# A two-layer hybrid backbone step on one core: pre-norm by channel slices, split output-projection weights kept in SBUF, weight splits on VectorE alone, and new rules for the order

## The chip, the core and the metric

One core of a Trainium2 chip runs the whole step in one launch. The metric is device time in microseconds (us). Engines are named as in the profile: PE is TensorE (matmuls and transposes; PEld its weight loads), DVE is VectorE, ACT is ScalarE, POOL is GpSimd, SP is SyncE, which issues the DMA transfers of the weights.

## What is computed

640 tokens (512 latent tokens of a sample, 128 of a prompt) of width 1024 go through two layers. In the reference, cut to what matters here:

```python
def modulate(x, g, shift, scale):
    return rms_norm(x, g) * (1.0 + scale) + shift

for l in range(2):
    # silu(c) @ w_mod[l] + b_mod[l], cut into six sections of 1024, for sample and prompt
    mod = split(silu(c) @ w_mod[l] + b_mod[l], 6)
    h = modulate(x, norm_mix_pre[l], mod[0], mod[1])
    # layer 0: attention and Hyena on the columns of h @ w_in, joined, then @ w_out
    # layer 1: mLSTM heads, forward and backward, gated, then @ w_out
    out = mixer(h)
    x = x + mod[2] * rms_norm(out, norm_mix_post[l])
    h = modulate(x, norm_ffn_pre[l], mod[3], mod[4])
    # conv_ffn: gelu(conv(h @ w_up)[:, :2816]) * conv(h @ w_up)[:, 2816:], then @ w_down
    x = x + mod[5] * rms_norm(conv_ffn(h), norm_ffn_post[l])
```

Prompt and sample share the weights; the prompt has modulation values of its own. All is float32.

## The kernel before

**Products of split operands.** A float32 product is taken as three products of fp32r operands: each operand x is split into h, x rounded to fp32r, and l = x - h; the matmuls are h·h, l·h and h·l (`SPLIT3`, line 386). So each weight slice needs a cast (`wh`, on ACT) and a subtraction (`wl`), and each activation likewise (`a1h`, `a1l` before the first FFN; `o0h`, `o0l` before layer 0's output projection; `hh`, `hl` before a down-projection). `split` makes the pair.

**Two forms of projection.** `fm_task` and `fm_head` compute 128 output channels for all tokens, with the weight slice stationary (the up-projection of the FFN, the mLSTM's inputs): eight contraction slices k, 384 early tokens and 256 late ones. `fm_head` (line 412) begins such a phase: the early tokens of the first five outputs, then their late ones. `tm_tasks` (line 500) computes tokens by 1024 outputs, for two groups of token tiles in turn, `HALVES` = tiles 0, 1, 2, then tiles 3, 4 (a tile is 128 tokens): for each contraction slice a 512 KB weight slice is loaded, split and multiplied with each tile of the group. The last three slices (`KEEP_`) of the first group are done tile by tile and stay for the second, which begins with them; the others are loaded and split again. The output projections (eight slices) and down-projections (22 slices) have this form.

**The boundary.** When a group of a projection is done, `boundary` (line 889) is spawned as a side chain, marked urgent. It squares each tile on ACT with the sum read out, multiplies it by the modulation gate on DVE, takes the inverse root by small integer and float steps on DVE (128 by 3 elements), and adds the residual on DVE. Then `pre_norm` (line 803) normalizes again (another square and inverse root), scales each tile's row (`xn`), transposes it in blocks of 128 by 128 on PE (four to a PSUM bank), and for each block scales and shifts by channel (half on DVE, half on ACT), casts (half on DVE, half on ACT) and subtracts on POOL, all in pieces of 128 by 128. The up-projection's first matmul needs tiles 0, 1, 2 complete. A row buffer for tile 4 is one that tile 0's pre-norm has given back (line 900).

**Modulation.** `mod_section` computes a section from w_mod in 512 KB loads with ACT, DVE and POOL adding products; its `finish` folds the partitions: two DMAs, two additions on POOL (`modf`), then matmuls of two columns that add up and transpose (`modt`). Layer 1's sections 0, 1, 3, 4 and layer 0's section 5 are spawned in layer 0's FFN once hidden slice `J0` = 5 is there.

**What sets the order.** The program is emitted by a planner (`Order`, line 60). Tasks on streamed weights follow one another; side chains (boundaries, modulation, attention, Hyena, the mLSTM heads) are woven in where an estimate of each engine's time says that their operands are ready. `Lane.cost` (line 244) estimates each instruction, `issue` (line 117) keeps the engines' clocks, with 125 ns between a result and its reader on any engine. `prefetch` (line 1820) places the weights' loads and splits, one task ahead; while an urgent chain is open it gives `wl` to POOL where POOL would be free before DVE (line 1836). The three PSUM tiles `mm` and two banks `aux` are taken and given back by the same planner.

All engine calls but matmuls and transposes are recorded under one helper line, 263; matmuls are line 343, transposes line 352.

Of the kernel before, what the change touches and what calls it, by code (L numbers as in the profile page):

```python
# [18 lines left out]
P = 128  # L19
D = 1024  # L20
# [19 lines left out]
# columns of the packed per-channel vectors  # L40
# [19 lines left out]
class Order:  # L60
    """Program order. Tasks on streamed weights follow one another; side chains are woven in between, by an
    estimate of when each engine gets to an instruction and of when its operands are there. A chain yields
    nothing (go on when what it has issued is finished), a time, keys that it needs, or a PSUM tag."""

    LAT = 125.0
    TICK = 10240.0 / 3
    WARM = 1275.0
# [5 lines left out]
    def __init__(self):  # L73
# [8 lines left out]
        self.ticks = {}  # L82
        self.after = None
# [11 lines left out]
    # ---- engines  # L95
# [21 lines left out]
    def issue(self, eng, cost, outs, ins, lat=0.0, rows=1.0):  # L117
        t = max(self.t[eng], self.avail(ins) + self.LAT)
        for o in outs + [i for i in ins if str(i.space) == "PSUM"]:
            x = self.last.get(o.name)  # L120
            if x is not None and x[1] != eng:
                t = max(t, x[0] + self.LAT)
        if eng == "PE":
            q = int(t // self.TICK)
            self.ticks[q] = self.ticks.get(q, 0.0) + cost * rows
# [4 lines left out]
        f = e + lat  # L130
        for o in outs:
# [10 lines left out]
    # ---- chains  # L142
# [61 lines left out]
    def until(self, t):  # L204
        """Chains that can go on before t."""
# [16 lines left out]
    # ---- PSUM  # L222
# [15 lines left out]
class Lane:  # L238
    """An engine whose instructions are also put on the estimate."""
# [4 lines left out]
    def cost(self, op, outs, ins):  # L244
        n = 1
        for d in max(outs + ins, key=lambda a: a.free_size()).shape[1:]:
            n *= d
        psum = any(str(a.space) == "PSUM" for a in outs + ins)
        if self.key == "DVE":
            if op in ("tensor_scalar", "tensor_copy") and not psum:  # L250
                return 0.52 * n + 70 + (60 if len(ins) > 1 else 0)
            return 1.04 * n + (130 if psum else 70)
        if self.key == "ACT":
            return 0.833 * n + 95 + (145 if len(ins) > 1 else 0)
        if op == "tensor_tensor":
            return 2.3 * n + 25
        return 1.05 * n + 25

    def __getattr__(self, op):
        f = getattr(self.engine, op)  # L260

        def call(*args, **kw):
# [5 lines left out]
            if op == "dma_start":  # L268
# [3 lines left out]
                self.od.dma = max(self.od.dma, self.od.t["SP"], self.od.avail(ins)) + n / 400.0  # L272
                f_ = self.od.dma + 2000.0
# [7 lines left out]
            self.od.issue(self.key, self.cost(op, outs, ins), outs, ins)  # L281
# [1787 lines left out]
```

## Time and profile before

| | |
|---|---|
| device time, median of 3 runs | 1798.43 us (1796.11 to 1804.24) |
| profiled execution, first to last instruction | 1802.8 us |
| PE busy | 1716.3 us (95%), 10132 instructions |
| DVE busy | 1255.4 us (70%), 2052 instructions |
| ACT busy | 783.4 us (43%), 1287 instructions |
| POOL busy | 528.8 us (29%), 358 instructions |
| moved by DMA | 208.08 MB, mean 115 GB/s |

The profiled execution has no time of its own beside its span in the record; 1802.8 us lies between the median and the slowest of the three runs. Busy shares are means over stages: an engine at 70% can be what another waits for in a stretch of some microseconds. Times in the rows below are from the start of the span. A row of the timeline gives start, duration, engine, line, operation, result and operands, size, count, and in brackets how long the engine had been idle and what ended that. Matmuls overlap, so a row with x2 gives the time of both. The granted clock (PEclk) is a share of TensorE's full speed.

### The profile page before, as it was taken

The numbers are of one execution on the slowest core, as the hardware profiler recorded it, in microseconds if no ns is written. First come the engines' busy times: TensorE is split into PE (matmuls) and PEld (weight loads), VectorE is DVE, ScalarE is ACT, GpSimd is POOL, SyncE is SP. The second block draws the span as 40 slices with busy tenths as digits, with TensorE's granted clock in tenths as the row PEclk, the third lists the DMA queues.
The fourth block names the chain that finished last, engine by engine and source line by source line (L and its number), as shares of the span: only waits on it lengthen the run. The fifth ranks groups of instructions, "written<-read, shape, count | busy, mean of one in ns | idle before, by whom it ended". The sixth has DMA issues, their size and how long they took to land. (4 is left out here: it accounts for less than half of the span.)

```text
span 1802.8 us, 25891 instructions
## 1 busy us (share of the span) xinstructions
PE 1716.3 (95%) x10132; PEld 1550.6 (86%) x10132; DVE 1255.4 (70%) x2052; ACT 783.4 (43%) x1287; POOL 528.8 (29%) x358
## 2 busy tenths in 40 slices
PE   7989998998999999989899999999989999999998
PEld 3687896778999999968688999999779999998876
DVE  6777887765677798874765897787568744445465
ACT  5443235645444454433545443434465432323343
POOL 1244423125245564530612221111164412111010
PEclk9999999999999999989899999999999999999999
DMA  8334243222244444542344221212224322223343
GB/s 296 131 132 138 82 132 120 71 87 77 95 141 163 145 148 141 178 161 90 124 142 135 87 87 54 71 54 68 92 85 166 115 71 75 79 71 107 127 152 129
DMA packets 64948, 208.08 MB, mean 115 GB/s; under 512 B 7287, under 2 KB 12407, under 8 KB 64826
## 3 DMA queue, kind: packets, MB, share of 16 engines
q1 hardware_dynamic: 64826, 206.43, 34.0%
q8 instruction: 80, 1.31, 0.3%
q14 instruction: 42, 0.34, 0.1%
HBM read 200.36 MB, written 3.94 MB: 113 GB/s over the span
## 5 line engine op out<-in xcount | busy, mean ns | idle before, releaser
L263 DVE TENSOR_TENSOR wl<-wr,wh 128x1024 fp32r<-128x1024 f32 x245 | 319.8, 1307 | 151.9 <-ACT wh L263 151.8
L263 ACT CAST wh<-wr 128x1024 fp32r<-128x1024 f32 x268 | 279.8, 1046 | 226.9 <-PE dn L343 133.1
L263 POOL TENSOR_TENSOR acc<-acc,modp 128x1024 f32<-128x1024 f32 (+1 forms) x84 | 200.5, 2394 | 191.2 <-ACT modp L263 191.1
L263 POOL TENSOR_TENSOR hid<-zg,zu 128x640 f32<-128x640 f32 x44 | 106.0, 2408 | 304.1 <-DVE zu L263 304.0
L263 DVE SCALAR_TENSOR_TENSOR acc<-mw,sc,acc 128x1024 f32<-128x1024 f32 x70 | 147.9, 2113 | 17.5 <-DMA mw<-in_w_mod 16.9
L263 DVE SCALAR_TENSOR_TENSOR zg<-g,vec,zg 128x127 f32<-128x127 f32 (+3 forms) x168 | 87.3, 541 | 87.6 <-ACT zg L263 84.6
L263 POOL TENSOR_TENSOR wl<-wr,wh 128x1024 fp32r<-128x1024 f32 x23 | 56.4, 2453 | 303.6 <-ACT wh L263 297.4
L343 PE MATMUL dn<-wh,hl 128*128 128x512 f32 x440 | 140.6, 400 | 4.8 <-DVE hl L263 4.8
L343 PE MATMUL dn<-wl,hh 128*128 128x512 f32 x440 | 140.9, 401 | 3.5 <-POOL wl L263 3.5
L343 PE MATMUL dn<-wh,hh 128*128 128x512 f32 x440 | 141.1, 401 | 1.1 <-ACT hh L263 0.6
L263 DVE SCALAR_TENSOR_TENSOR zu<-u,vec,zu 128x511 f32<-128x511 f32 (+2 forms) x164 | 86.7, 549 | 79.5 <-ACT zu L263 76.6
L263 ACT ACTIVATE modp<-mw,sc 128x1024 f32<-128x1024 f32 (+1 forms) x84 | 83.6, 1009 | 117.3 <-DMA mw<-in_w_mod 66.4
L343 PE MATMUL u<-a1l,wh 128*128 128x384 f32 (+1 forms) x336 | 105.2, 313 | 3.1 <-POOL a1l L263 3.1
L343 PEld LDWEIGHTS dn<-wh,hl 128*128 128x128 f32 x440 | 83.6, 191 | 26.5 <-DVE hl L263 7.1
L343 PE MATMUL u<-a3l,wh 128*128 128x384 f32 (+1 forms) x336 | 104.5, 311 | 1.6 <-POOL a3l L263 1.6
L343 PE MATMUL u<-a1h,wl 128*128 128x384 f32 (+1 forms) x336 | 105.1, 313 | 0.4 <-DVE wl L263 0.4
L343 PE MATMUL g<-a1h,wh 128*128 128x384 f32 (+1 forms) x336 | 105.3, 313 | 0.0
L343 PE MATMUL g<-a1l,wh 128*128 128x384 f32 (+1 forms) x336 | 105.1, 313 | 0.0
L343 PE MATMUL u<-a1h,wh 128*128 128x384 f32 (+1 forms) x336 | 104.9, 312 | 0.0
L343 PE MATMUL g<-a1h,wl 128*128 128x384 f32 (+1 forms) x336 | 104.9, 312 | 0.0
L343 PEld LDWEIGHTS dn<-wl,hh 128*128 128x128 f32 x440 | 84.2, 192 | 24.0 <-POOL wl L263 4.4
L343 PE MATMUL u<-a3h,wl 128*128 128x384 f32 (+1 forms) x336 | 104.3, 310 | 0.4 <-DVE wl L263 0.4
(744 smaller groups left out, 4713.8 us busy)
## 6 DMA issues: line engine op xcount, KB each, us to landing
wr<-in_w_up SPq DMA_DIRECT2D x92, 512.0 KB, 3.6
wr<-in_w_down SPq DMA_DIRECT2D x82, 512.0 KB, 3.2
mw<-in_w_mod SPq DMA_DIRECT2D x80, 512.0 KB, 4.4
wr<-in_w_ml SPq DMA_DIRECT2D x34, 512.0 KB, 3.3
wr<-in_w_out SPq DMA_DIRECT2D x26, 512.0 KB, 3.3
wr<-in_w_in SPq DMA_DIRECT2D x13, 512.0 KB, 3.5
wr<-in_w_u SPq DMA_DIRECT2D x12, 512.0 KB, 3.1
we<-in_w_mod SPq DMA_DIRECT2D x8, 512.0 KB, 5.0
```

The lines of the kernel that those rows point to most:

```text
L263: r = f(*args, **kw)
L343: r = nc.tensor.matmul(out, lhsT, rhs, start=start, stop=stop)
```

## The change

- **Weight splits.** All `wl` go to DVE; the choice of POOL is gone from `prefetch`.
- **Output projections.** The activation is split once for all 640 tokens (`whole`), not once per group. Slices 0 to 4 in layer 0 and 2 to 4 in layer 1 (`STAY`) are split into pages of 512 columns that stay for the second group (`away`), so with the three that stayed before, layer 0 loads its eight slices once, and layer 1 loads two again. 26 loads of w_out become 18.
- **Pre-norm.** Rows are scaled in halves of 512. Then, per channel slice k, all tiles of the group are transposed to one bank and scaled, cast and subtracted as one piece of 384 or 256 columns: even k scaled on DVE, cast on ACT, subtracted on DVE; odd k scaled on ACT, cast on DVE, subtracted on POOL. Each slice is announced by itself, and the first task of the up-projection waits slice by slice (`needs`). For the first group, slice k from 3 on waits until a slice of the output projection that holds its pages is used (`FREE`).
- **Boundary.** Tile 4's row is taken from the pool `mw`, without waiting for tile 0.
- **Modulation.** `finish` lets 8000 ns pass in the estimate (`FOLDED`) between the fold on POOL and its matmuls. `J0` goes from 5 to 1.
- **mLSTM heads.** Output gates come 3 heads later, not 2 (`LAG`); of the values 2, not 3, come late (`VLAG`).
- **Order.** The estimate has new costs, a latency apart from the occupancy, a wake-up time per engine in place of 125 ns, a port that DVE and POOL take in turn for instructions on SBUF operands, and slower transfers.

Calls are recorded under lines 278, 359 and 370 now. The diff, cut:

```diff
-    LAT = 125.0
+    WAKE = {"PE": 55.0, "DVE": 40.0, "ACT": 40.0, "POOL": 80.0}
...
+        self.port = {"DVE": 0.0, "POOL": 0.0}
...
-    def issue(self, eng, cost, outs, ins, lat=0.0, rows=1.0):
-        t = max(self.t[eng], self.avail(ins) + self.LAT)
+    def issue(self, eng, cost, outs, ins, lat=0.0, act=0.0, shared=False):
+
+        t = self.avail(ins)
...
+        t = max(self.t[eng], t + self.WAKE.get(eng, 0.0))
+        if shared:
+            t = max(t, self.port["POOL" if eng == "DVE" else "DVE"])
...
+        if shared:
+            self.port[eng] = f
...
-            return 1.04 * n + (130 if psum else 70)
+            d = (0.52 if fast else 1.04) * n + 150 + 62 * ptrs
+            return (d + 25, 0, False) if op in ("tensor_reduce", "reciprocal") else (d - 85, 85, fast or len(near) > 1)
...
-            return 2.3 * n + 25
-        return 1.05 * n + 25
+            return 2.16 * n + 100, 70, True
+        return 1.0 * n + 15, 70, op != "memset"
...
-    def fm_part(out, w, act, c0, c1):
+    def fm_part(out, w, act, c0, c1, needs=None):
...
+            if needs is not None:
+                od.need([(*needs, k)])
...
-                old = g > 0 and n < KEEP
+                old = g > 0 and (n < KEEP or k in away)
+                mine = g == 0 and n in stay
+                if mine:
+                    away.add(k)
...
+                                od.ready.add((name, "used", m))
...
                 yield
+                yield FOLDED
                 yield "aux"
                 pt = aux(f"modt{l}{s}")
...
+        for c in (slice(0, 512), slice(512, D)):
+            for j, i in enumerate(tiles):
+                if j % 2:
+                    nc.scalar.mul(xn[i][:, c], xs[i][:, c], r[:, j : j + 1])
+                else:
+                    nc.vector.tensor_scalar(xn[i][:, c], xs[i][:, c], r[:, j : j + 1], None, op0=ALU.mult)
...
+        for k in range(KT):
+            yield "aux"
+            ps = aux(f"{name}t{k}")
+            for j, i in enumerate(tiles):
+                TR(ps[:, j * P : (j + 1) * P], xn[i][:, k * P : (k + 1) * P])
+            if pages is not None and tiles[0] == 0 and k >= FREE:
+                yield [(pages, "used", min(KT - 1, k - FREE + 3))]
...
+            split(h[:, c], low[:, c], y, nc.gpsimd if k % 2 else nc.vector,
+                  nc.vector.tensor_copy if k % 2 else nc.scalar.copy)
+            od.ready.add((key, l, tiles[0], k))
+            yield 0
...
             if nxt is not None and i >= ROWS:
-                yield [(key, l + (s == 5), i - ROWS)]
-            t[i] = row(f"{name}t{i}")
+                t[i] = mw.tile([P, D], F32, tag="mw", name=f"{name}t{i}")
+            else:
+                t[i] = row(f"{name}t{i}")
...
-            c0, c1 = halves[g][0] * P, halves[g][-1] * P + P
-            hh, hl = page(f"{name}h{k}{g}", FR), page(f"{name}l{k}{g}", FR)
-            split(hh[:, 0 : c1 - c0], hl[:, 0 : c1 - c0], mix[order[k]][:, c0:c1])
-            cur[g, k] = hh, hl
+            hh, hl = page(f"{name}h{k}", FR), page(f"{name}l{k}", FR)
+            split(hh[:, 0:T], hl[:, 0:T], mix[order[k]][:, 0:T])
+            cur[k] = hh, hl
...
-    LAG, VLAG = 2, 3
+    LAG = 3
+    VLAG = 2
...
-    J0 = 5
+    J0 = 1
...
-            slow = not od.urgent or max(od.t["POOL"], at) + POOLX > max(od.t["DVE"], at)
-            split(h, l, t.raw, nc.vector if slow else nc.gpsimd)
-            t.w = (h, l)
+            if t.away:
+                t.w = [[page(f"w{x}{q}{c}", FR)[:, 0:512] for c in range(2)] for x in "hl"]
+                for c in range(2):
+                    split(t.w[0][c], t.w[1][c], t.raw[:, c * 512 : c * 512 + 512])
+            else:
+                t.w = [wp.tile([P, 1024], FR, tag=f"w{x}", name=f"w{x}{q}") for x in "hl"]
+                split(*t.w, t.raw)
```

Three places show what the order becomes. First GpSimd's queue at the boundary between layer 0's output projection and its FFN (`acc` is a modulation section's sum, `wl` a weight split, `a1l` an activation split, `o0p0ny` a scaled block of the first group and `o0p3ny` of the second). Before:

```order
L263 TENSOR_TENSOR acc_2096<-acc_2096,modp_2097 128x1024 x3
L263 TENSOR_TENSOR wl_3199<-wr_3016,wh_3198 128x1024
L263 TENSOR_TENSOR wl_3223<-wr_3044,wh_3222 128x1024
L263 TENSOR_TENSOR wl_3248<-wr_3072,wh_3247 128x1024
L263 TENSOR_TENSOR wl_3287<-wr_3206,wh_3286 128x1024
L263 TENSOR_TENSOR a1l_3141<-o0p0ny_3337,a1h_3140 128x128
L263 TENSOR_TENSOR a1l_3143<-o0p0ny_3337,a1h_3142 128x128
```

With the change:

```order
L278 TENSOR_TENSOR a1l_3304<-o0p0ny_3305,a1h_3303 128x384
L278 TENSOR_TENSOR a1l_3336<-o0p0ny_3337,a1h_3335 128x384
L278 TENSOR_TENSOR a1l_3368<-o0p0ny_3369,a1h_3367 128x384
L278 TENSOR_TENSOR a1l_3406<-o0p0ny_3407,a1h_3405 128x384
L278 TENSOR_TENSOR a1l_3304<-o0p3ny_3555,a1h_3303 128x256
```

The four weight splits are gone from this queue, and four pieces per group stand where 24 and 16 stood.

Second, TensorE's queue at the same boundary (`o_3`, `o_4` are the output projection's tiles 3 and 4, `o0p0nt` the transposes of the first group). Before, with the second group's matmuls around the first transposes:

```order
L343 MATMUL o_4_3191<-wh_3247,o0l_3252 128x512 x2
L343 MATMUL o_4_3191<-wl_3248,o0h_3251 128x512 x2
L352 MATMUL o0p0nt_3332<-ident,o0p0t_3159 128x128 x4
L343 MATMUL o_3_3168<-wh_3286,o0h_3290 128x512 x2
L343 MATMUL o_3_3168<-wh_3286,o0l_3291 128x512 x2
L343 MATMUL o_3_3168<-wl_3287,o0h_3290 128x512 x2
```

With the change:

```order
L359 MATMUL o_3_3160<-wl_2914,o0h_2920 128x512
L359 MATMUL o_3_3160<-wl_2915,o0h_2920 128x512
L370 MATMUL o0p0nt_3289<-ident,o0p0t_3151 128x128
L370 MATMUL o0p0nt_3289<-ident,o0p0t_3154 128x128
L370 MATMUL o0p0nt_3289<-ident,o0p0t_3157 128x128
L370 MATMUL o0p0nt_3299<-ident,o0p0t_3151 128x128
L370 MATMUL o0p0nt_3299<-ident,o0p0t_3154 128x128
L370 MATMUL o0p0nt_3299<-ident,o0p0t_3157 128x128
L359 MATMUL o_4_3183<-wh_2912,o0h_2920 128x512
```

One tile's four blocks stood together, after 72 matmuls of tiles 3 and 4; now three tiles' blocks of one slice stand together, two slices at a time, after 66.

Third, TensorE's queue early in layer 0's down-projection (`dn_0` to `dn_2` are its first group's tiles, `modt` a modulation section's fold). Before:

```order
L343 MATMUL dn_1_6639<-wh_6484,hl_6489 128x512 x2
L343 MATMUL dn_1_6639<-wl_6485,hh_6488 128x512 x2
L343 MATMUL modt_6646<-vec,modf_6519 128x2 x8
L343 MATMUL dn_2_6664<-wh_6484,hh_6488 128x512 x2
L343 MATMUL dn_2_6664<-wh_6484,hl_6489 128x512 x2
```

With the change:

```order
L359 MATMUL dn_2_6555<-wh_6592,hl_6597 128x512 x2
L359 MATMUL dn_2_6555<-wl_6593,hh_6596 128x512 x2
L359 MATMUL modt_6676<-vec,modf_6519 128x2 x8
L359 MATMUL dn_0_6541<-wh_6620,hh_6624 128x512 x2
L359 MATMUL dn_0_6541<-wh_6620,hl_6625 128x512 x2
```

The fold's matmuls stood inside the down-projection's first slice; they stand behind its fifth now.

## Rows read from the trace of the kernel before

**Rows 1.** The page's first table: busy us (share of the span) and instructions.

```profile
PE 1716.3 (95%) x10132; PEld 1550.6 (86%) x10132; DVE 1255.4 (70%) x2052; ACT 783.4 (43%) x1287; POOL 528.8 (29%) x358
```

**Rows 2.** The per-core line: span and mean granted TensorE clock.

```profile
core 0: 1802.8 us, clock 0.977
```

**Rows 3.** Stretches: us, busy us (instructions) of PE, PEld, DVE, ACT, POOL, PEclk, DMA, GB/s.

```profile
380.00:435.00 55.00, 46.02 (x211) 38.96 (x210) 39.19 (x87) 29.26 (x58) 28.51 (x30) 0.91 0.29 96
672.00:682.00 10.00, 7.71 (x52) 7.29 (x51) 9.17 (x12) 4.89 (x6) 4.76 (x2) 1.00 0.16 54
786.00:826.00 40.00, 33.22 (x135) 27.16 (x134) 19.38 (x20) 9.84 (x14) 6.08 (x2) 0.87 0.39 117
850.00:945.00 95.00, 84.72 (x377) 68.28 (x375) 67.80 (x118) 49.29 (x88) 36.29 (x33) 0.95 0.39 129
1294.00:1330.00 36.00, 28.42 (x127) 21.45 (x126) 30.74 (x62) 22.75 (x48) 21.09 (x28) 0.95 0.36 116
1375.00:1640.00 265.00, 265.00 (x1810) 264.24 (x1809) 148.61 (x204) 91.76 (x106) 67.45 (x28) 1.00 0.27 92
75.00:200.00 125.00, 113.57 (x632) 104.93 (x631) 91.26 (x109) 52.14 (x89) 57.13 (x37) 0.93 0.40 136
```

**Rows 4.** TensorE's waits by releaser: total us, times, longest us.

```profile
PE modt L343 <- POOL modf L263: 7.2, 2, 6.8
...
PE o L343 <- DVE o0l L263: 3.8, 4, 1.7
...
PE dn L343 <- POOL wl L263: 3.5, 2, 3.3
...
PE u L343 <- POOL a1l L263: 3.1, 1, 3.1
```

**Rows 5.** VectorE's timeline at layer 0's boundary: start us, us, instruction.

```profile
382.56 2.27 DVE L263 SCALAR_TENSOR_TENSOR o0p0q<-o0p0a,o0p0q 128x3 f32<-128x3 f32 x1
...
385.32 3.35 DVE L263 SCALAR_TENSOR_TENSOR x<-o0p0t,o0p0y,x 128x1024 f32<-128x1024 f32 x1
388.60 0.41 DVE L263 TENSOR_TENSOR o0l<-vx,o0h 128x256 fp32r<-128x256 f32 x1
388.94 2.47 DVE L263 SCALAR_TENSOR_TENSOR x<-o0p0t,o0p0y,x 128x1024 f32<-128x1024 f32 x2
...
396.74 0.16 DVE L263 SCALAR_TENSOR_TENSOR o0p0ny<-o0p0na,o0p0ny 128x3 f32<-128x3 f32 x1
...
401.72 0.74 DVE L263 TENSOR_SCALAR o0p0t<-x,o0p0ny 128x1024 f32<-128x1024 f32 x1
402.39 1.21 DVE L263 TENSOR_TENSOR wl<-wr,wh 128x1024 fp32r<-128x1024 f32 x1
...
412.03 1.37 DVE L263 TENSOR_SCALAR o0p0ny<-o0p0nt,mod,mod 128x128 f32<-128x128 f32 x4 [1.09 <-PE o0p0nt L352]
```

**Rows 6.** GpSimd's timeline in the same stretch.

```profile
382.40 2.40 POOL L263 TENSOR_TENSOR wl<-wr,wh 128x1024 fp32r<-128x1024 f32 x1 [45.19 <-ACT wh L263]
385.18 2.42 POOL L263 TENSOR_TENSOR wl<-wr,wh 128x1024 fp32r<-128x1024 f32 x1 [0.38 <-ACT wh L263]
...
409.15 11.11 POOL L263 TENSOR_TENSOR a1l<-o0p0ny,a1h 128x128 fp32r<-128x128 f32 x20 [0.70 <-ACT a1h L263]
```

**Rows 7.** TensorE's timeline in the same stretch.

```profile
402.88 1.05 PE L343 MATMUL o<-wl,o0h 128*128 128x512 f32 x2
...
408.22 0.63 PE L343 MATMUL o<-wh,o0l 128*128 128x512 f32 x2
...
413.23 0.60 PE L352 MATMUL o0p0nt<-ident,o0p0t 128*128 128x128 f32 x4
```

**Rows 8.** The page's costliest groups: busy us, mean ns, idle before and its releaser.

```profile
L263 DVE TENSOR_TENSOR wl<-wr,wh 128x1024 fp32r<-128x1024 f32 x245 | 319.8, 1307 | 151.9 <-ACT wh L263 151.8
...
L263 POOL TENSOR_TENSOR wl<-wr,wh 128x1024 fp32r<-128x1024 f32 x23 | 56.4, 2453 | 303.6 <-ACT wh L263 297.4
```

**Rows 9.** ScalarE's timeline: the square that begins the chain.

```profile
379.02 1.02 ACT L263 ACTIVATE o0p0j<-o 128x1024 bf16<-128x1024 f32 x1 [3.07 <-PE o L343]
```

More of the change, by code (lines that the diff above doesn't have):

```diff
@@ L441, in run @@
                 held = w is None
[L442 removed]
+                yield from fm_part(pl[:, 0 : T - CUT], st[n, "w"] if held else w, act, CUT, T,
+                                   needs_b if n == back[0] else None)
                 if held and RB:
@@ L498, in fm_first, with tm_tasks, cols, flat @@
         return [take(n) for n in range(3)] + [Task(all_)]
-    def tm_tasks(lhs, src, nk, groups, name, finish, prep=None, needs=lambda k, g: (), single=False, tail=False, own=None, subs=(), more=()):
-        out, held = [], {}
-        KEEP = KEEP_ + bool(more)
+    def tm_tasks(lhs, src, nk, groups, name, finish, prep=None, needs=lambda k, g: (), single=False, tail=False, own=None, stay=(), whole=False):
+        out, held, away = [], {}, set()
+        def cols(w, c):
+            return w[c] if isinstance(w, list) else w[:, c * 512 : c * 512 + 512]
+        def flat(w):
+            return [x for y in w for x in (y if isinstance(y, list) else [y])]
         def group(g, order):
@@ L531, in run @@
                         held[k] = w
-                    if n == nk - 1 and not last and prep is not None:
+                    if n == nk - 1 and not last and prep is not None and not whole:
                         for m in range(nk - 1, nk - 1 - KEEP, -1):
@@ L560, in run @@
                             finish(pss[i], i)
-                        elif n == nk - 1:
-                            for sub in subs or [tiles]:
-                                if i == sub[-1]:
-                                    finish({x: pss[x] for x in sub}, sub)
+                        elif n == nk - 1 and i == tiles[-1]:
+                            finish(pss, tiles)
                     if old:
-                        release(bool(more) and n == KEEP - 1)
-                spare = bool(more) and g == 0 and n == nk - KEEP
-                return Task(run, None if old else src(k), prep=None if prep is None or old else (lambda: prep(k, g)),
-                            keys=list((own or needs)(k, g)) + list(more) * spare, hold=n >= nk - keep, spare=spare)
+                        release(k in away)
+                    if last and n < nk - 1:
+                        od.ready.add((name, "used", n))
+                return Task(run, None if old else src(k), prep=None if prep is None or old or g and whole else (lambda: prep(k, g)),
+                            keys=list((own or needs)(k, g)), hold=n >= nk - keep or mine, away=mine)
             return [make(n) for n in range(nk)]
@@ L797, in spawn_mods, with pre_norm @@
         return Task(run)
-    def new_act(name):
-        return [(page(f"{name}h{k}", FR), page(f"{name}l{k}", FR)) for k in range(KT)]
-    def pre_norm(xs, tiles, l, s, act, name, key, xn):
+    def pre_norm(xs, tiles, l, s, act, name, key, xn, pages):
         n = len(tiles)
@@ L887, in hybrid_step, with boundary @@
     ROWS = 4
-    def boundary(pss, tiles, l, s, xs, nxt, name, key):
+    FREE = 3
+    STAY = ((0, 1, 2, 3, 4), (2, 3, 4))
+    def boundary(pss, tiles, l, s, xs, nxt, name, key, pages=None):
         n = len(tiles)
@@ L915, in boundary @@
             return
-        yield from pre_norm(xs, tiles, l + (s == 5), 3 if s == 2 else 0, nxt, name + "n", key, t)
+        yield from pre_norm(xs, tiles, l + (s == 5), 3 if s == 2 else 0, nxt, name + "n", key, t, pages)
     def finish_last(pss, tiles, l, xs):
@@ L1822, in prefetch @@
         done = False
-        while state["split"] < len(wt_tasks) and (state["live"] < BUFS or wt_tasks[state["split"]].spare):
+        while state["split"] < len(wt_tasks) and (state["live"] < BUFS or wt_tasks[state["split"]].away):
             q = state["split"]
```

151 lines of the change are left out of this document (69 added, 82 removed).

## The prediction

> **What bounds the kernel now.** I read the page's first table and the per-core line first [rows 1, 2]: TensorE is busy 1716.3 of 1802.8 us, at a mean granted clock of 0.977. It is the bound, and the change neither adds nor removes a matmul or a transpose: only their order differs. So what can be won is TensorE's idle time, 1802.8 - 1716.3 = 86.5 us, and its time at the lower of its two clock levels (1.2 instead of 2.4 GHz; a mean of 0.977 costs at most 0.023 x 1802.8 = 41.5 us). The ceiling is 128 us. All sums are made against this execution's 1802.8 us; the median of the runs is 1798.43, 4.4 us less, and I take that off at the end. About 0.5% (9 us) is what a measurement of this kernel can tell from no change.
>
> Where do the 128 us lie? The view by stretches answers [rows 3]. In the second FFN's up-projection (1375 to 1640) TensorE is busy all of 265.00 us at clock 1.00: nothing to win. Five short stretches hold what this change speaks of. I charge each with its idle time plus (1 - clock) x its length:
>
> - output projection to FFN, layer 0 (380 to 435): 9.0 + 0.09 x 55 = 14.0 us;
> - a gate section's broadcast (672 to 682): 2.3 us;
> - the fold of a modulation section (786 to 826): 6.8 + 5.2 = 12.0 us;
> - FFN to layer 1 (850 to 945): 10.3 + 4.7 = 15.0 us;
> - output projection to FFN, layer 1 (1294 to 1330): 7.6 + 1.8 = 9.4 us.
>
> Together 52.7 us. The third view, TensorE's waits, names who ended them [rows 4]: GpSimd's half of the fold (modf), VectorE's half of a split operand (o0l), GpSimd's (wl, a1l).
>
> **Why VectorE is late there.** Put its timeline beside GpSimd's [rows 5, 6]. At 382.40 GpSimd starts a weight split that takes 2.40 us. VectorE's next small step with two SBUF inputs, 128x3, takes 2.27 us; such steps take 0.16 elsewhere. At 385.18 the next split starts, and a 128x1024 residual takes 3.35 us, where two of them take 2.47 later, so 1.24 each. Each time VectorE gets through only when GpSimd's instruction is over: about 2 us lost per weight split, and there are four in this boundary, so 8 us. TensorE then waits for VectorE, and behind that idle time two 128x512 matmuls take 1.05 us together, where they take 0.63 a little later [rows 7]: the lower clock level. Last, the first up-projection matmul waits 3.1 us for a1l [rows 4]: GpSimd does 20 of the 128x128 activation splits one behind the other in 11.11 us [rows 6].
>
> **The change, part by part.**
>
> *GpSimd's weight splits go to VectorE.* Before: 23 on GpSimd at 2453 ns, 245 on VectorE at 1307 ns [rows 8]. After: 252 whole ones and 16 halves, all on VectorE: 260 for 268, since layer 0's output projection keeps all eight slices and layer 1's six, so 8 of 26 loads of w_out go, with their ACT and VectorE splits. VectorE gets 15 more; an unblocked one takes 1.21 us [rows 5], so +18 us. Cover: VectorE has 15.8, 27.2 and 5.3 us free in the three boundary stretches [rows 3], and gets back some 8 us at the first by not being blocked. The 8 loads win nothing: DMA is busy 0.29 to 0.39 there and TensorE waits for none.
>
> *The pre-norm by channel slices.* Per boundary, 40 scale-and-shift, 40 casts and 40 GpSimd splits of 128x128 become 24, 16 and 16 wider pieces, half of the splits on VectorE. No row has a 128x384 scale from PSUM; four of 128 take 1.37 us [rows 5], so it lies between 0.34 and 1.03. I take 0.6. VectorE's split of 384 columns lies on the line through 256 (0.41) and 1024 (1.21): 0.55. GpSimd's lies between one of 128 (11.11 / 20 = 0.56) and three (1.67); I take 0.9, the weight split's 2453 ns x 384/1024.
>
> *The chain that TensorE needs, layer 0.* Count from the end of tile 2's last matmul: square 1.0 [rows 9] and its read-out 0.2 (as a small step), product with the gate 1.2 (as a weight split of that size), eleven small steps at 0.16, 1.8, three residuals at 1.24, 3.7, three weight splits at 1.21 that the new order puts between, 3.6, eleven small steps again, 1.8, two half rows at 0.37 (a whole one takes 0.74), 0.7 [rows 5]: 14.0 us. Ahead of the first transposes the new order puts 66 matmuls of tiles 3 and 4, at 0.23: 15.2 us. (The 1810 matmuls of 1375 to 1640, half of 384 columns and half of 256, take 265.00 us [rows 3]; that is 0.146 for 320 columns and 0.23 for 512.) The chain fits with 1.2 us to spare. From there to the first up-projection matmul stand 30 matmuls and 24 transposes, at 0.15 each since four take 0.60 [rows 7]: 30 x 0.23 + 24 x 0.15 = 10.5 us, 2.6 per pair of slices; a pair costs VectorE 0.6 + 0.55 + a cast of 0.3 (0.74 x 384/1024, as a scaled row [rows 5]) = 1.5, so it keeps up. The last slice is the worst: its pages come free only when the output projection's last matmul is done, and two squares on ACT and two gate products on VectorE (1.2 each) stand ahead of its own steps, so about 5 us until a1l is split, against 7 slices of three matmuls of 384 columns, 0.53 us each, 3.7 us, that TensorE has meanwhile. About 1.3 us of wait is new. I leave 2 us: 12 of 14 come back.
>
> *The other boundaries.* In layer 1 two slices are still loaded again, and slices 6 and 7 are transposed between the up-projection's first matmuls: I leave 2.4 of 9.4, so 7 back. After the first FFN the chain has 22 slices of 12 matmuls, 2.8 us each, as cover, and VectorE needs 1.21 + 0.41 = 1.6 us per slice for the splits: 11 of 15 back.
>
> *The fold waits 8 us more before its transposing matmuls.* TensorE stood 6.8 us in one piece for modf [rows 4], with ready matmuls behind it in its own queue. 8 us is more than 6.8: 11 of 12 back. Behind the moved step waits only the modulation of a pre-norm that comes later.
>
> *Layer 1's modulation starts after hid 1, not hid 5.* Its 40 loads of 512 KB, each with a VectorE, an ACT and a GpSimd step, move ahead of four pairs of up-projections on every queue, SP's too. The up-projection alone leaves VectorE 116 of 265 us, and DMA is at 0.27 [rows 3]. Cost nothing; without that cover an up-projection would wait for its convolution.
>
> *What else the new rules reorder* (Hyena, attention, mLSTM; output gates three heads later): no step is added. The ceiling has 75 us there, 11.4 + 8.8 = 20 of them between 75 and 200 [rows 3]. Bounds: those 20 back, or 15 lost (six new waits as long as a GpSimd split, 2.4 [rows 6]). The new rules let VectorE and GpSimd wait for each other, as rows 5 and 6 show, and the old ones don't; I take 5 back. Of the gate broadcast's 2.3, 1.3.
>
> Sum: 12 + 7 + 11 + 11 + 5 + 1.3 = 47 us. 1802.8 - 47 - 4.4 = 1751: **I predict 1751 us.**
>
> **Rivals.**
>
> *A. The block stays, in smaller pieces.* GpSimd still splits 4 slices per group. If each takes 1.67 us and VectorE, whose casts and splits come between, stands still for all of it, 6.7 us come back as delay, with a last slice that is later for it about 9 us in each of the two short boundaries: 18 of 47 lost, 1769 us. For it: rows 5 and 6. Against it: VectorE's scale steps from PSUM took 1.37 for four beside GpSimd's splits (412.03, inside the 11.11 us), so that part of its work isn't stopped. The Trainium skill's page "SBUF — State Buffer", section "SBUF: two separate sides", says that VectorE and GpSimd hold one shared port pair as an exclusive lock for a whole instruction; this trace agrees for steps with two SBUF inputs. That speaks against leaving any split on GpSimd, and by it the time would be this rival's.
>
> *B. The reordered middle gives all its 20 us*, 15 more than I took: 1736 us. Against it: VectorE is busy 91 of 125 us there, and needed.
>
> *C. The stall only moves* (waits as large as the old ones, for a later slice at each boundary and for the fold at its new place, and the middle gives nothing): within 9 us of 1798.
>
> *D. Slower: VectorE becomes the bound at the boundaries.* It gets 15 weight splits (18 us) and 24 activation splits (12 of 0.55, 12 of 0.41: 11.5 us) and loses some 8 us of small casts: +21 us. It decides where VectorE's work exceeds the stretch: in layer 1 it fills 30.7 of 36 us already. If nothing comes back of what GpSimd seems to take from it, all 21 us are TensorE's, and only the fold gains: 1802.8 + 21 - 11 - 4.4 = 1808 us. Against it: 8 of VectorE's 39.2 us in the first boundary are plainly blocked time.
>
> **How the numbers follow.** Forecast 0.58, A 0.15, B 0.13, C 0.06, D 0.08. Faster by over 0.5%: forecast, A and B, 0.86; same 0.06; slower 0.08. The range leaves out C and D (0.14): its lower end is B with all of the 52.7 us, 1736 - 10 = 1726; its upper end is A with the middle losing 15, 1769 + 15 = 1784.
>
> **What would show it.** Right: VectorE's small steps near 0.16 us at the boundaries; no wait of TensorE over 1 us for o0l, hl, wl or modf; clock 1.00 in the five stretches; TensorE busy near 97%. Wrong: GpSimd's 384-column splits above 1.5 us with VectorE rows stretched beside them (A); VectorE over 90% busy at a boundary and TensorE waiting for wl (D); new waits in attention or the mLSTM heads.

## The result, and the profile after

The changed kernel takes 1774.81 us (median of 4 runs, 1771.78 to 1778.59) against 1799.68 for the kernel before in the same comparison: a ratio of 0.9867, 95% interval 0.9845 to 0.9889. That is faster by 1.3%, inside the range given, 24 us from the 1751 forecast and half of the gain that it stood for. The two profiled executions are further apart than the medians: 1802.8 and 1770.0 us, 32.8 us, since the one of before lies above its median and the one of after below. What follows splits these 32.8 us.

The page's first table and the per-core line of the changed kernel, which answer to [rows 1, 2]:

```profile
PE 1702.6 (96%) x10132; PEld 1542.7 (87%) x10132; DVE 1246.2 (70%) x2035; ACT 765.3 (43%) x1214; POOL 438.3 (25%) x239
```

```profile
core 0: 1770.0 us, clock 0.984
```

To see where the time went, cut both traces at the same work: TensorE's first matmul of layer 0's output projection, the 200th gate matmul of its FFN, the first and last of its down-projection, and the same in layer 1 (first of the output projection, 200th gate matmul). The view by stretches at these points, before (columns as in [rows 3]):

```profile
0.00:341.00 341.00, 308.41 (x1607) 245.07 (x1607) 260.31 (x434) 153.88 (x307) 110.49 (x74) 0.95 0.40 138
341.00:493.30 152.30, 142.28 (x776) 126.85 (x777) 95.00 (x186) 72.92 (x130) 45.57 (x50) 0.96 0.28 94
493.30:741.50 248.20, 245.45 (x1666) 244.44 (x1665) 203.30 (x218) 109.59 (x120) 128.65 (x50) 0.99 0.44 147
741.50:926.20 184.70, 169.99 (x717) 135.19 (x716) 120.32 (x146) 84.08 (x134) 59.63 (x41) 0.94 0.43 142
926.20:1255.00 328.80, 321.17 (x2313) 315.60 (x2311) 261.56 (x590) 146.16 (x285) 65.49 (x63) 0.99 0.25 80
1255.00:1399.50 144.50, 136.48 (x771) 121.40 (x770) 103.85 (x183) 73.53 (x128) 58.01 (x56) 0.99 0.34 115
```

and after:

```profile
0.00:353.30 353.30, 313.05 (x1609) 245.96 (x1609) 270.00 (x437) 156.17 (x308) 112.99 (x74) 0.95 0.39 133
353.30:488.00 134.70, 133.94 (x776) 121.80 (x776) 96.84 (x177) 67.70 (x104) 25.35 (x15) 1.00 0.30 103
488.00:730.90 242.90, 242.90 (x1666) 242.55 (x1665) 195.07 (x212) 105.30 (x116) 126.22 (x46) 1.00 0.41 138
730.90:892.30 161.40, 160.26 (x717) 129.34 (x716) 117.22 (x146) 80.48 (x118) 30.18 (x14) 1.00 0.50 166
892.30:1226.10 333.80, 322.85 (x2312) 316.58 (x2311) 261.57 (x599) 149.61 (x288) 54.94 (x49) 0.99 0.24 79
1226.10:1366.40 140.30, 135.41 (x772) 122.43 (x771) 91.36 (x168) 62.48 (x95) 26.98 (x17) 0.98 0.28 95
```

PE's counts agree to within two matmuls in each pair, so the differences are time for the same work. Layer 0's mixer: 12.3 us **longer**. Layer 0's boundary: 17.6 shorter. The up-projection: 5.3 shorter. The down-projection, with the fold and most of its boundary: 23.3 shorter. Layer 1's mixer: 5.0 **longer**. Layer 1's boundary: 4.2 shorter. The rest is equal to 0.4 us. So 50.4 us came back and 17.3 were lost.

TensorE's waits by releaser after, to be put beside [rows 4] (the longest, then one at layer 1's boundary and one of the mLSTM's gates):

```profile
PE hyp L359 <- DMA hyw<-in_hy_w: 6.3, 1, 6.3
PE s L359 <- ACT p L278: 4.7, 1, 4.7
PE xt L370 <- DVE xa L278: 4.3, 1, 4.3
PE pt L370 <- DVE rr L278: 3.9, 3, 1.3
...
PE u L359 <- DVE a3h L278: 2.9, 1, 2.9
...
PE colp L370 <- DVE wi L278: 1.9, 1, 1.9
```

None of the four waits of [rows 4] is left among them. The first row was there before as well (6.2 us). The others belong to attention (s, pt), the first normalization (xt), the mLSTM's gates (colp), and one slice of layer 1's pre-norm (a3h).

VectorE at layer 0's boundary after, to be put beside [rows 5]:

```profile
392.45 0.16 DVE L278 SCALAR_TENSOR_TENSOR o0p0y<-o0p0a,o0p0y 128x3 f32<-128x3 f32 x1
392.65 1.28 DVE L278 SCALAR_TENSOR_TENSOR x<-o0p0t,o0p0y,x 128x1024 f32<-128x1024 f32 x1
393.85 1.22 DVE L278 TENSOR_TENSOR wl<-wr,wh 128x1024 fp32r<-128x1024 f32 x1
394.99 2.48 DVE L278 SCALAR_TENSOR_TENSOR x<-o0p0t,o0p0y,x 128x1024 f32<-128x1024 f32 x2
397.38 2.35 DVE L278 TENSOR_TENSOR wl<-wr,wh 128x1024 fp32r<-128x1024 f32 x2
```

The small steps take 0.16, a residual 1.28 where one took 3.35, and the three weight splits stand between as the order had it. In the 55 us from 353.3 on, TensorE is busy for all 55.00 at clock 1.00.

### The profile page after: what moved, and what is told of

Read it like the earlier page. It is cut to its first block, busy times and chain, and to the rows that moved or that the text cites. A ratio compares the mean times of both kernels' runs of the same rounds, so it can differ in the third digit from the quotient of the medians.

```text
span 1770.0 us, 25662 instructions
## 1 busy us (share of the span) xinstructions
PE 1702.6 (96%) x10132; PEld 1542.7 (87%) x10132; DVE 1246.2 (70%) x2035; ACT 765.3 (43%) x1214; POOL 438.3 (25%) x239
## 4 chain that ended last, share of the span: by engine, by line
PE 84%; DVE 9%; issue 3%; ACT 2%; DMA 1%; POOL 1%; SPq 0%; DVEq 0%; ACTq 0%; POOLq 0%
PE u L359 20%; PE dn L359 17%; PE g L359 17%; PE o L359 6%; PE mk L359 3%; PE mo L359 3%; PE mq L359 3%; PE qkv L359 2%; PE mv L359 2%; DVE wl L278 1%; PE po L359 1%; PE mod L359 1%; PE modt L359 1%; PE s L359 1%; DVE qsq L278 1%
## 5 line engine op out<-in xcount | busy, mean ns | idle before, releaser
L278 DVE TENSOR_TENSOR wl<-wr,wh 128x1024 fp32r<-128x1024 f32 (+1 forms) x268 | 333.8, 1250 | 139.1 <-ACT wh L278 138.8
L278 ACT CAST wh<-wr 128x1024 fp32r<-128x1024 f32 (+1 forms) x268 | 272.2, 1019 | 173.5 <-PE dn L359 109.5
L278 POOL TENSOR_TENSOR acc<-acc,modp 128x1024 f32<-128x1024 f32 (+1 forms) x84 | 206.1, 2462 | 211.3 <-ACT modp L278 211.0
L278 DVE SCALAR_TENSOR_TENSOR acc<-mw,sc,acc 128x1024 f32<-128x1024 f32 x70 | 152.1, 2172 | 4.2 <-DMA mw<-in_w_mod 3.8
L359 PE MATMUL u<-a3h,wh 128*128 128x384 f32 (+1 forms) x336 | 105.6, 314 | 2.9 <-DVE a3h L278 2.9
L359 PE MATMUL g<-a3h,wh 128*128 128x384 f32 (+1 forms) x336 | 104.9, 312 | 0.0
L359 PE MATMUL g<-a3l,wh 128*128 128x384 f32 (+1 forms) x336 | 104.6, 311 | 0.0
L359 PE MATMUL g<-a3h,wl 128*128 128x384 f32 (+1 forms) x336 | 104.4, 311 | 0.0
```

The lines of the kernel that those rows point to most:

```text
L278: r = f(*args, **kw)
L359: r = nc.tensor.matmul(out, lhsT, rhs, start=start, stop=stop)
```

## The experiments

Eighteen kernels ran. Ratios are to the kernel before, in the same comparison, each with its 95% interval; the changed kernel's is 0.9867 (0.9845 to 0.9889). The changed kernel is called C here, the kernel before B. B's own median lay between 1797.7 and 1803.4 us in these comparisons, so between kernels of different comparisons the ratios say more than the times.

**GpSimd's weight splits, by themselves.** In B, one edit:

```diff
-            slow = not od.urgent or max(od.t["POOL"], at) + POOLX > max(od.t["DVE"], at)
+            slow = True or max(od.t["POOL"], at) + POOLX > max(od.t["DVE"], at)
```

> The kernel before, with one edit: the 23 weight splits of GpSimd go to VectorE, nothing else. Theory 1 (GpSimd's splits hold VectorE up, about 2 us each, and that is a main part of the boundaries' cost): 8 us back at layer 0's boundary and about as much at the others together, so some 12 us below the kernel before, 1787 us. Theory 2 (VectorE has no room there, the slices and the kept weights did the work): VectorE gets 23 splits of 1.2 us in the short stretches and nothing is won: 1799 us or up to 10 slower.

Measured 1776.75 us, 0.9878 (0.9854 to 0.9903): 23 us, twice what theory 1 gave it, and as much as the whole change. But it is not the same gain. Nopool's stretches at layer 0's boundary and at the down-projection, between the same points:

```profile
337.70:482.40 144.70, 136.86 (x777) 123.86 (x778) 94.71 (x192) 72.52 (x130) 28.93 (x44) 0.98 0.30 99
729.70:902.60 172.90, 164.94 (x717) 132.84 (x716) 112.24 (x153) 83.40 (x134) 38.34 (x34) 0.97 0.45 151
```

These are 7.6 and 11.8 us below B; with the up-projection (247.3) and layer 1's boundary (142.7) it is 22.1 us, where C has 50.4. The wait for modf is still there (6.1 us). The rest of the change adds 28.3 us at these places, and C loses most of them again in the two mixers (353.3 and 333.8 us, in nopool 337.7 and 324.8). And the other way round, in C, with GpSimd allowed again (36 splits go there now, not B's 23):

```diff
-                split(*t.w, t.raw)
+                at = max(od.t["ACT"], od.avail([t.raw])) + 950.0
+                slow = not od.urgent or max(od.t["POOL"], at) > max(od.t["DVE"], at)
+                split(*t.w, t.raw, nc.vector if slow else nc.gpsimd)
```

> The changed kernel, with GpSimd's weight splits allowed again by the rule of the kernel before (it takes 36 of them now; the kept weights stay on VectorE). Theory 1 (the weight splits on GpSimd were the main cost of the boundaries and nothing else in the change makes up for it): it gives back most of what taking them off alone won (22.9 us), so 1790 to 1800 us. Theory 2 (the new estimate knows the shared port and the slices need less of VectorE, so the splits do little harm): within 8 us of 1775.

Measured 1805.36 us, 1.0014 (0.9994 to 1.0034): with these splits on GpSimd nothing is left of the gain. The rest of the change still keeps 20 us at the boundaries, the up-projection and the down-projection (145.0, 242.9, 177.8 and 144.0 us), and loses as much in the mixers and behind the last of these points. The trace shows what the splits do. The tiles hl and wl in the second group of layer 0's down-projection, 850 to 925 us (duration in ns min/median/max, first and last start in us), in poolback:

```profile
L278 DVE TENSOR_TENSOR hl<-hid,hh x18: 409/2421/2639, 849.8 to 914.9; 128x256 fp32r<-128x256 f32 x18
```

```profile
L278 POOL TENSOR_TENSOR wl<-wr,wh x15: 2357/2402/3342, 854.8 to 924.7; 128x1024 fp32r<-128x1024 f32 x15
```

VectorE's subtraction of 256 columns takes 0.41 us alone, and 2.42 at the median where GpSimd splits weights beside it: it lasts as long as GpSimd's instruction. TensorE's waits for hl in the whole trace (0.6 us in C):

```profile
PE dn L359 <- DVE hl L278: 14.0, 8, 3.5
```

The Trainium skill's page "SBUF — State Buffer", section "SBUF: two separate sides", calls this an exclusive lock held for the whole instruction, and not a share of bandwidth; 2.42 us beside 2.40 agrees.

**GpSimd's remaining activation splits** (rival A). In C, `split(h[:, c], low[:, c], y, nc.vector, ...)` for all slices.

> The changed kernel, with the pre-norm's subtractions of odd slices on VectorE instead of GpSimd (12 of 384 and 12 of 256 columns). Theory 1 (GpSimd's pieces of 1.0 us are short and hold nobody up at a cost): the time stays within 5 us of 1775, VectorE has 11.5 us more work. Theory 2 (rival A of the prediction: the block stays in smaller pieces and costs 9 us in each of two boundaries): 5 to 15 us faster than 1775.

Measured 1781.23 us, 0.9891 (0.9873 to 0.9909): not faster, and rival A falls. In C, GpSimd's piece of 384 columns takes 1.0 us in seven of the eight at these boundaries, and VectorE's rows between such pieces keep their length (a3l 0.56, a3h 0.36).

**The new estimate in layer 0's mixer.** mixold is C with the old costs, latency and transfers until the first matmul of the output projection; mixnew is B with the new ones until there. In both, TensorE's instructions up to that matmul stand in the order of the other kernel.

```diff
+        self.old = True
...
+                    if name == "o0" and g == 0 and n == 0:
+                        od.old = False
```

> The changed kernel, but layer 0's mixer (all up to the first output-projection matmul) is ordered by the old estimate, so that this stage has exactly the instruction order of the kernel before; everything behind it as in the change. Theory 1 (the new estimate made layer 0's mixer slower, 353.3 us to its end against 341.0 in the two profiles, and that is where my forecast of 5 us back failed): the stage ends near 341 and the time is 12 us below the changed kernel's, about 1763 us. Theory 2 (the 12 us are scatter between two executions, or come from what the change does to buffers): the stage stays near 350 and the time near 1775.

> The kernel before, with the new estimate for layer 0's mixer alone, so that this stage has the changed kernel's order. Theory 1: the stage ends near 353, the time is 12 us above the kernel before, about 1811 us. Theory 2: near 1799 us.

mixold: 1760.77 us, 0.9777 (0.9758 to 0.9796). mixnew: 1811.90 us, 1.0079 (1.0055 to 1.0103). Both as theory 1 has it, 14 us one way and 12 the other. The stretch up to the output projection in mixold, then in mixnew:

```profile
0.00:342.70 342.70, 309.49 (x1606) 245.66 (x1606) 260.65 (x435) 154.30 (x307) 110.44 (x74) 0.95 0.40 137
```

```profile
0.00:350.60 350.60, 311.33 (x1607) 244.78 (x1608) 267.22 (x436) 155.68 (x307) 108.85 (x74) 0.95 0.39 134
```

**Which rule of it?** Four kernels undo one rule each in that stretch of C: the shared port, the latency, the durations, the transfers.

> The changed kernel, but in layer 0's mixer alone the estimate doesn't let VectorE and GpSimd wait for each other; its other new rules stay. Theory 1 (this one rule pushes the side chains of Hyena and attention back, so that TensorE's independent matmuls are used up before attention needs them as cover): attention's first score matmul comes nearer to 276 us, the stage ends near 343, time about 1764 us. Theory 2 (the rules act together; any new order of this stage is a new draw): the stage ends within 5 us of 353 or worse, time near 1775.

> The changed kernel, but in layer 0's mixer alone each result is estimated to reach its reader after 125 ns, as before, instead of 40 to 80 ns and a latency; its other new rules stay. Theory 1 (one rule of the new estimate costs layer 0's mixer its 12 us, and it is this one): the stage ends near 341 us instead of 353, time about 1763 us. Theory 2 (the rules cost together, as any other order would): within 6 us of 1775.

> The changed kernel, but in layer 0's mixer alone the durations on VectorE, ScalarE and GpSimd are estimated as before; its other new rules stay. Theory 1 (the new durations are the rule that costs the 12 us): the stage ends near 341 us, time about 1763 us. Theory 2 (the rules cost together): within 6 us of 1775.

> The changed kernel, but in layer 0's mixer alone transfers are estimated at 400 bytes per ns and 2.0 us, as before, instead of 300 and 1.9. Theory 1 (the slower transfers move the first stage, where TensorE waits 4.3 us for the normalized input and runs at half clock behind it: 70.0 us against 64.3): that stage goes back to 64 us, time about 1769 us. Theory 2 (the rules cost together): within 6 us of 1775, the stage near 70.

No one rule carries it. noport 1781.13 us, 0.9868 (0.9837 to 0.9900); nowake 1779.91, 0.9870 (0.9855 to 0.9885); oldcost 1789.11, 0.9922 (0.9907 to 0.9937); olddma 1789.64, 0.9923 (0.9907 to 0.9940). The stretch ends at 360.3, 352.6, 363.3 and 364.6 us in these, at 353.3 in C and at 341.0 in B. olddma's first stage did go back to 64 us, as its theory 1 had it, but by the last qkv matmul this was gone (242.2 us, in C 242.1), and attention's stage behind it took 122.4 us for C's 111.2. That oldcost and olddma come out slower than C, neither theory had. One rival was not tried alone: mixold also undoes the estimate's new rules for TensorE's own durations and clock, which none of these four touch.

**What stands beside attention.** In C two products of Hyena's output gate lie on GpSimd where attention's first softmax waits for VectorE. VectorE and GpSimd in C:

```profile
281.13 4.69 DVE L278 TENSOR_TENSOR acc<-acc,modc 1x512 f32<-1x512 f32 x2
285.86 2.45 DVE L278 SCALAR_TENSOR_TENSOR acc<-mw,sc,acc 128x1024 f32<-128x1024 f32 x1
```

```profile
280.90 2.39 POOL L278 TENSOR_TENSOR acc<-acc,modp 128x1024 f32<-128x1024 f32 x1 [8.44 <-ACT modp L278]
283.25 3.97 POOL L278 TENSOR_TENSOR vx<-zh,vx 128x640 f32<-128x640 f32 x2
```

vxdve is C with these four products on VectorE (`nc.vector.tensor_tensor(vx[i][:, 0:T], ...)`).

> The changed kernel, with the four products of Hyena's output gate (tile vx, 128x640) on VectorE instead of GpSimd. Two of them stand beside attention's first softmax in the changed kernel, where a VectorE pair of 1x512 takes 4.69 us against 1.27 in the kernel before. Theory 1 (GpSimd's side work, put beside attention by the new estimate, stretches VectorE there, and that is the loss of layer 0's mixer): the stage from the last qkv matmul to the first output-projection matmul, 111.2 us, falls by 5 or more, time about 1769 us. Theory 2 (the loss is that attention's chain has no other matmuls beside it): within 3 us of 1775.

Measured 1768.99 us, 0.9810 (0.9767 to 0.9853), 6 us below C. The pair takes 1.27 us there:

```profile
279.31 1.27 DVE L278 TENSOR_TENSOR acc<-acc,modc 1x512 f32<-1x512 f32 x2
```

But the stage from the last qkv matmul fell only by 2.9 us, from 111.2 to 108.3, less than the 5 that theory 1 asked for, and the two ratios' intervals overlap a little. The eight kernels with C's TensorE order up to the output projection have 109.3 to 112.3 us for this stage and each a wait of 4.7 us at s; vxdve has 1.8 us there. The six with B's order have 100.3 to 101.7 us, so most of the mixer's loss lies in this stage, and the block is a part of it, not all.

**The old estimate throughout** (allold: C ordered by the old estimate from start to end).

> The changed kernel with the old estimate throughout; slices, kept weights, VectorE's weight splits and all else stay as in the change. Theory 1 (the new estimate only costs, in both mixers: 12 us in layer 0's, and some 9 us between the first FFN's end and the second output projection, where nopool took 324.8 us and the changed kernel 333.8): 1750 to 1755 us, below mixold's 1761. Theory 2 (the new estimate is what makes the boundaries and the fold smooth, and it loses in layer 0's mixer by chance): above mixold, 1765 to 1780 us.

Measured 1775.11 us, 0.9848 (0.9805 to 0.9892): theory 2. It wins 15 us in layer 0's mixer (338.2 us) and gives 8.0 back at layer 0's boundary, 5.4 in the up-projection and 2.8 at layer 1's boundary. The new estimate as a whole is worth nothing here.

**The fold.** fold0 is C without `yield FOLDED`; j5fold0 has `J0 = 5` besides.

> The changed kernel without the 8000 ns between the fold and its matmuls. Theory 1 (the delay by itself removes the wait of 6.8 us and the low clock behind it): the stage of layer 0's first down-projection group, 96.0 us in the changed kernel and 106.2 before, goes back to about 106, the time to about 1785 us. Theory 2 (the new estimate of GpSimd's durations places the fold late enough): within 3 us of 1775.

> The changed kernel without the 8000 ns and with layer 1's modulation starting after hidden slice 5, as before. In fold0 the stage of the down-projection's first group kept its 96.0 us without the delay. Theory 1 (the earlier start, J0 = 1, makes the fold come early enough): the stage goes to about 105 us, time about 1783 us. Theory 2 (the new estimate of GpSimd's durations does it): the stage stays at 96 us, the time within 4 us of fold0's 1770.

fold0: 1770.48 us, 0.9805 (0.9766 to 0.9845). Theory 1 fell: the down-projection's stretch is 161.3 us without the delay and 161.4 with it. j5fold0: 1783.19 us, 0.9895 (0.9853 to 0.9938), and 171.1 us for that stretch, as theory 1 expected in size, though the loss lies in the second group (74.5 us for 65.3) and not in the first: the fold's matmuls stand between the two groups there, and TensorE waits 3.7 us for modf. So with the earlier start of layer 1's modulation the delay isn't needed, and without both the wait is back. Whether the delay alone would do wasn't tried.

**Layer 1's mixer.** lag2 is C with `LAG, VLAG = 2, 3` as before.

> The changed kernel with the output gates two heads later and three late values, as before. Theory 1 (the 9 us lost in layer 1's mixer come from the new estimate): within 3 us of the changed kernel's 1775. Theory 2 (they come from the heads' new order): about 1766 us.

Measured 1781.41 us, 0.9877 (0.9825 to 0.9929): no gain. The stretch is 344.2 us against C's 333.8, so the heads' new order wins there. scan corrects one duration of the estimate in C, that of the gates' scans:

```diff
+            if "scan" in op:
+                return 2.15 * n + 25, 85, True
```

> The changed kernel, with one duration of the estimate corrected by the trace: the gates' scans on VectorE (8x640: 1.48 us, 8x512: 1.25, 8x128: 0.39) are taken as 2.15 ns per element, where the new estimate has 1.04. Theory 1 (layer 1's mixer loses 5 us because TensorE meets the transposes colp in its queue before VectorE's gate chain is done, waits 2.5 us in two pieces and runs at half clock behind them, 945.8 to 952.7): colp stands later, the stretch from the first FFN's last matmul to the first mq matmul, 66.0 us, falls by 4 or more, time about 1770 us. Theory 2 (the loss lies in the other parts of that mixer): within 3 us of 1775.

Measured 1767.03 us, 0.9804 (0.9758 to 0.9850): theory 1, though this interval and C's touch. In C, TensorE's gate transposes by the view of their tile (ns min/median/max, first and last start; the last line is TensorE's wait before them), then in scan:

```profile
L370 PE MATMUL colp<-ident,wi x5: 236/304/304, 944.9 to 949.3; 40*128 40x40 f32 x5
...
  DVE wi L278: 1.9, 1
```

```profile
L372 PE MATMUL colp<-ident,wi x5: 228/229/232, 950.6 to 954.0; 40*128 40x40 f32 x5
```

They stand 4.4 us later, counted from the FFN's last matmul, TensorE no longer waits at them, and from the FFN's last matmul to the first mq matmul it is 60.7 us at clock 1.00, where C has 66.0 at 0.95:

```profile
893.60:954.30 60.70, 57.06 (x400) 54.92 (x398) 42.19 (x80) 37.38 (x62) 8.76 (x17) 1.00 0.36 119
```

```profile
892.30:958.30 66.00, 60.52 (x402) 58.02 (x401) 42.38 (x82) 38.30 (x64) 8.43 (x17) 0.95 0.35 116
```

**Layer 1's boundary.** In C the cast of the first group's last slice stands on VectorE behind the second group's inverse root and a residual:

```profile
1290.77 1.29 DVE L278 SCALAR_TENSOR_TENSOR x<-o1p3t,o1p3y,x 128x1024 f32<-128x1024 f32 x1
1291.98 0.35 DVE L278 CAST a3h<-o1p0ny 128x384 fp32r<-128x384 f32 x1
```

TensorE waits 2.95 us for that cast, and runs slower behind the wait (0.53 for a matmul of this size that takes 0.34 just before it):

```profile
1292.38 0.69 PE L359 MATMUL u<-a3h,wh 128*128 128x384 f32 x1 [2.95 <-DVE a3h L278]
1292.87 0.53 PE L359 MATMUL u<-a3h,wl 128*128 128x384 f32 x1
```

mixold_lc is mixold with this in `boundary`, before the inverse root:

```diff
+        if nxt is not None and tiles[0] and s == 2:
+            yield [(key, l, 0, KT - 1)]
```

> As mixold, and the second group's inverse root and residuals at an output-projection boundary wait until the first group's last slice is announced, so that VectorE's cast of slice 7 (tile a3h) no longer stands behind them (at layer 1 it comes 3 us late in the changed kernel, TensorE waits 2.9 us for it and then runs at half clock for a few us; the stage from the output projection's last matmul to the second group's last transpose loses 9.5 us). Theory 1 (that queue order is the rest of layer 1's boundary cost): the stage's loss falls from 9.7 to about 3, time 6 us below mixold's 1761, about 1755 us. Theory 2 (the last slices are late anyway, as their pages come free with the last matmul): within 2 us of mixold.

Measured 1755.31 us, 0.9716 (0.9678 to 0.9753): theory 1. The stretch from the output projection's last matmul on, mixold_lc, then C:

```profile
1264.70:1342.30 77.60, 76.24 (x516) 74.38 (x515) 61.41 (x112) 38.68 (x60) 23.22 (x14) 1.00 0.29 98
```

```profile
1283.30:1366.40 83.10, 78.22 (x516) 76.07 (x515) 60.56 (x112) 38.62 (x60) 24.14 (x14) 0.96 0.27 92
```

**Put together.** best is mixold_lc with vxdve's edit, best2 is mixold_lc with scan's.

> As mixold_lc (old estimate in layer 0's mixer, second group's steps at a boundary behind the first group's last slice), with the four products of Hyena's output gate on VectorE. Theory 1 (GpSimd's side work stretches VectorE beside attention in any order of this stage): the last stage of the mixer, 100.5 us there, falls by 3 or more, time about 1750 us. Theory 2 (in the old order GpSimd's products lay where they held nobody up, so VectorE only gets more work): 1755 us or up to 5 more.

> As mixold_lc, with the corrected duration of the gates' scans. Theory 1: 4 us below mixold_lc's 1755, about 1751 us. Theory 2: within 3 us of 1755.

best: 1762.91 us, 0.9776 (0.9761 to 0.9791), theory 2: what won 6 us in the new order wins nothing in the old one. Not all of its loss need be the products': layer 1's mixer came out in another order too, 336.2 us for mixold_lc's 331.7. best2: 1749.88 us, 0.9707 (0.9667 to 0.9747), 25 us below C and, in its own comparison, 53 below B, though from mixold_lc it can't be told apart by its interval. It is the fastest of all that ran:

```profile
PE 1692.3 (97%) x10132; PEld 1533.2 (88%) x10132; DVE 1246.0 (71%) x2035; ACT 764.4 (44%) x1214; POOL 442.5 (25%) x239
```

## Where the prediction was right, and where it failed

**Right: the block.** VectorE stands still while GpSimd splits weights (2.42 us for 0.41), and taking these splits away gives 23 us by itself (nopool); giving 36 of them back takes the whole gain away (poolback). The prediction saw this mechanism. It isn't all that the change is worth: it is 22.1 of the 50.4 us at the places that the prediction spoke of. That nopool and C take the same time is chance, since the other 28.3 us and what C's mixers lose nearly cancel.

**Right: the boundaries, and somewhat more.** The terms for the boundaries, the fold and the gate's broadcast were 42 us. The four stretches that hold them gave 17.6 + 5.3 + 23.3 + 4.2 = 50.4. The stretches are wider than the prediction's five, and the two profiled executions lie 8 us further apart than the medians, so the excess of 8 us need not be the terms'. Layer 0's boundary was to keep 2 us; TensorE was busy for 133.94 of 134.70 us there. The unknown durations came out near what was taken: scale from PSUM 0.67 for 0.6, split of 384 columns 0.56 for 0.55, GpSimd's 1.0 for 0.9. At layer 1's boundary 4.2 us came back of the 7 forecast: the wait that was foreseen for the last slice at layer 0's boundary came here, by VectorE's queue order.

**Right in size, not in cause: the fold.** The term of 11 us rested on "8 us is more than 6.8". The wait is gone, but fold0 shows that the 8 us don't matter where J0 is 1. What does is that earlier start (j5fold0), which the prediction had put at nothing.

**Failed: "what else the new rules reorder".** This step took 5 us back, between bounds of 20 back and 15 lost, because the new rules let VectorE and GpSimd wait for each other and the old ones don't. Measured: 12.3 us lost in layer 0's mixer and 5.0 in layer 1's, 17.3 in all, a little beyond the bound. That is the size of the miss: without the two losses the median would be near 1757 us (an estimate, 1774.8 - 17.3), and the sum without the term gives 1756. The reason was the fault: it took a closer estimate for a better order. noport shows that undoing the port rule in that stretch wins nothing. Executions of one order differ by some us: B's order ends the stage between 335.4 and 342.7 us in six kernels that have it (B, nopool, allold, mixold, mixold_lc, best2), C's between 350.6 and 354.6 in eight. The orders with one rule undone end it between 352.6 and 364.6, none of them in the old range. What is shown of the loss is its place and size (mixold, mixnew) and a part of its mechanism: GpSimd's products beside attention (vxdve, 2.9 us less wait at s). The rest of the 12 us has no single cause among those tried, and stays open. In layer 1's mixer, what C's order loses by is shown: one duration of the estimate, 1.04 ns per element for scans that take more than 2, set the gate transposes ahead of their operands (scan, 5.3 us of the stage; the mixer takes 329.0 us there, as B's 328.8). But the old estimate had the same 1.04, B lost nothing by it, and allold, ordered by it throughout, takes 334.6 us in this mixer with that stage at clock 1.00. Which part of the change brought this loss is not shown.

**The range and the rivals.** The measured time lies in the range, but its upper end was added up wrongly: from 5 us back to 15 lost is 20 us, so A with that loss is 1789, not 1784. A's time, 1769, is the nearest, but its mechanism isn't what happened (subdve). B had the sign of the middle wrong, as the forecast had. C and D fell: no stall moved in its old size, and VectorE, with 96.84 of 134.70 us at layer 0's boundary, didn't become the bound. The prediction named new waits in attention or the mLSTM heads as what would show it wrong; they are what did.

## What to carry to other kernels

Look for an engine whose small steps last exactly as long as another engine's instruction, and try moving that other work by itself first: here this one edit took 23 us, as much as the whole change. When a change alters the rule by which a program is ordered, count every stage that the rule reaches as a term of unknown sign, as large as that stage's scatter between orders (here 335 to 365 us), and measure the stage with the old order kept, since that is one edit. The parts that won can then be kept without the ones that lost.

## What was not expected of the hardware

The block goes both ways, at these lengths: GpSimd's 384-column subtraction, 1.0 us otherwise, took 1.97 in poolback (from 420.69) while a 128x1024 residual ran on VectorE (420.52, 1.28 us), and 1.97 in C at layer 1's boundary (from 1292.41) beside another one (1292.24, 1.28 us), where TensorE waited 1.0 us for it. And it is not paid by VectorE's busy time alone: hl's 88 subtractions of the down-projections cost 97.5 us in poolback and 52.0 in C, 45.5 us more on VectorE, of which 14.0 us reached TensorE as waits for hl.
